# Key/value projection third, queries five tiles ahead, transposes moved, norm gains as rows, FFN2's first split behind the norm

## The chip, the cores and the metric

The kernel runs on one core of a Trainium2 chip. The metric is the device time of one execution in microseconds (us); three runs of the kernel before gave a median of 1015.74 us (1014.93 to 1016.44). The engines are TensorE (PE, its weight loads PEld), VectorE (DVE), ScalarE (ACT), GpSimd (POOL) and SyncE (SP), which here issues nearly all DMAs. Each engine works through its own instructions in order.

## The reference

One encoder layer over 512 tokens of width 1024, all in float32:

```
x = x + 0.5 * swiglu(rms_norm(x, ffn1_norm), gate1, up1, down1)     # width 2816
h = rms_norm(x, mix_norm);  P = h @ w_in                            # q, k, v of A and B
A: 8 heads of differential attention, two softmaxes each over 512 keys, + T5 bias, RMS norm
B: 8 query heads over 2 key/value heads, per-head RMS norm and rotary on q and k, softmax
x = x + concat(A, B) @ w_out
x = x + 0.5 * swiglu(rms_norm(x, ffn2_norm), gate2, up2, down2)
return rms_norm(x, final_norm)
rms_norm(x, g) = x * rsqrt(mean(x*x) + 1e-6) * g
```

## The kernel before

**Arithmetic.** Every large operand is split into two fp32r parts, hi (a cast on ScalarE) and lo (the difference, a subtraction on VectorE), and a product is three matmuls: hi by hi, hi by lo, lo by hi (`mm3`). A split of a weight block thus is ScalarE and VectorE work that has to be done before TensorE can use it; `Blocks` holds the list of weight blocks, loads them two ahead through SP (`load`) and splits them (`convert`, `get`). Evicting a transposed activation from PSUM is such a split too.

**Stages.** FFN1's gate/up products (0 to 246.7 us) go over 11 blocks of 256 columns; from the second on each product is made of seven smaller ones with sums of sub-blocks: of weights (T, on GpSimd and VectorE) and of activations (S1 to S4, `left_sums`). Then come FFN1's down product (to 366.4), the mix norm and the first projections (to 411), attention (to about 632), the output projection and FFN2's norm (to 660), FFN2's gate/up (to 884), down (to 1001) and the final norm.

**Norms.** A norm handles 128 tokens at a time: ScalarE's Square with its sum, VectorE and GpSimd for r, then z = x·r on VectorE (128x1024), eight transposes of 128x128 on TensorE per tile, into four PSUM banks, and the eviction of 128x256 pieces: hi with the column's gain as the scale on ScalarE, lo on VectorE. The gains of the three norms are loaded as columns (`gcol`, 4-byte elements) through SP at the start. `left_first` does the first 256 tokens, `left_second` the others.

**Attention.** 32 units of A and 32 of B, one for a head and 128 queries, named A0_0 to A7_3 and B0_0 to B7_3. The loop at the end of `build` takes one unit a step and is a software pipeline: scores of unit i (sA, sB), the join of softmax parts of unit i-1, the transposes of the weights (pt_A, pt_B) of unit i-3 (`LAG_T`), the product with v (poA, poB) of unit i-4 or i-5 (`LAG_V`), and for A the transposes of a head pair's output (ot) 7 units behind (`LAG_O`). The order of TensorE's instructions in the loop is that of the code. Between these steps `fill` puts other matmuls, "fillers", of which `FILLS` gives how many groups of three go to a step (one number for eight steps): first the projections in the order `FILL_ORDER`, then the output projection (po), which needs the ot tiles. For B, `B_heads` transposes a head's rotated queries (hT_q), splits them and copies them to the other 64 partitions by DMAs on SP (qh, ql), three steps ahead of the head's first unit; `make_k2` does the same for the keys (hT_k). The q and k of a head pair of A are copied into stacks (st) by small DMAs on SP. Outside the loop a scheduler orders the instructions of each engine by the code's order and by modelled costs; `tc.issue_after(x)` keeps instructions behind x.

Of the kernel before, what the change touches and what calls it, by code (L numbers as in the profile page):

```python
# [155 lines left out]
def build(ctx, tc, a, out):  # L156
# [100 lines left out]
    gcol = {}  # L257
    for nm in ("ffn1", "mix", "ffn2"):
        gcol[nm] = const.tile([P, NK], F32, name=f"gcol_{nm}")
        nc.sync.dma_start(out=gcol[nm], in_=a[f"{nm}_norm"][0].rearrange("(k p) -> p k", p=P))  # L260
        if nm == "ffn1":
            for t in (2, 3):
                nc.sync.dma_start(out=xn[t], in_=xv[:, t, :])
            blocks.load(2)
# [30 lines left out]
    def half_T(half, tags, tag, between=None, parts=2):  # L295

        ps = [bank(tags[kp], f"xt_{tag}{half}{kp}") for kp in range(4)]
        for i in range(2):
# [8 lines left out]
        return [(p.rearrange("p (k s) -> p k s", k=2)[:, e, :]) for p in ps for e in range(2)]  # L307

    def gained(hl, e, p, gain):

        last["act"] = nc.scalar.activation(hl[0][:, e, :], p, AF.Copy, scale=gain).ins
        last["dve"] = nc.vector.scalar_tensor_tensor(out=hl[1][:, e, :], in0=p, scalar=gain,
                                              in1=hl[0][:, e, :].bitcast(F32), op0=ALU.mult, op1=ALU.subtract).ins
# [4 lines left out]
    def left_first(g, tag, between=None, parts=2):  # L318

        ps = half_T(0, "DDBB", tag, between, parts)  # L320
# [738 lines left out]
```

## Time and profile before

| | |
|---|---|
| median of 3 runs | 1015.74 us (1014.93 to 1016.44) |
| profiled execution, its own time | 1015.6 us |
| span, first to last instruction | 1013.8 us |
[...]
| busy: PE, DVE, ACT, POOL | 974.1 (96%), 720.6 (71%), 489.0 (48%), 227.9 (22%) us |
| chain that ended last | PE 83%, DVE 6%, issue 3%, ACT 2%, DMA 2% |

TensorE is busy 96% of the span; the list of its waits and the timeline show the rest. A row of the timeline has the start, the duration, the engine, the line, the operation, its output and inputs and in brackets the idle time of the engine before it with what ended it. Line numbers are those of the kernel before.

### The profile page before, as it was taken

The page shows a single profiled execution, that of the slowest core. Times are in us where ns is not written, and L with a number is a line of the kernel's source. Part 1 is how long each engine was busy: PE and PEld are TensorE (multiplying, and loading weights), DVE is VectorE, ACT ScalarE, POOL GpSimd, SP SyncE. Part 2 cuts the span into 40 slices and gives each one's busy share as a digit, 9 for nine tenths or more (in the row PEclk, how much of TensorE's full clock was granted, in tenths as well). Part 3 has the DMA queues.
Part 4 walks back from the last instruction along what each step waited for, and adds up shares of the span by engine and source line. Part 5 has one row for each costly group of instructions (what it writes and reads, how often), then busy time and mean ns, then how long its engine had stood idle before and what let it go on. Part 6 is the DMA issues. An engine that isn't in the chain of part 4 may idle for free.

```text
span 1013.8 us, 16666 instructions
## 1 busy us (share of the span) xinstructions
PE 974.1 (96%) x6540; PEld 893.7 (88%) x6540; DVE 720.6 (71%) x1156; ACT 489.0 (48%) x845; POOL 227.9 (22%) x222
## 2 busy tenths in 40 slices
PE   7999999999999999999899989899999999999995
PEld 7999999999888888799888777699999999988884
DVE  5998899988232173777988886689999887842224
ACT  7555444445231162776766665574444454622213
POOL 1232223220000000122656442033222323000001
PEclk8999999999999999999999999999999999999998
DMA  8145534323223325545412121114433423233212
GB/s 244 52 127 188 179 108 126 116 93 109 99 83 106 102 79 144 139 116 158 136 54 58 27 63 52 43 42 125 126 103 106 126 83 125 84 111 118 83 42 83
DMA packets 82399, 105.45 MB, mean 104 GB/s; under 512 B 7873, under 2 KB 66753, under 8 KB 82321
## 3 DMA queue, kind: packets, MB, share of 16 engines
q1 hardware_dynamic: 81744, 103.35, 33.1%
q8 instruction: 51, 0.84, 0.4%
q10 hardware_dynamic: 576, 1.05, 0.3%
q14 instruction: 28, 0.22, 0.1%
HBM read 93.86 MB, written 6.32 MB: 99 GB/s over the span
## 4 chain that ended last, share of the span: by engine, by line
PE 83%; DVE 6%; issue 3%; ACT 2%; DMA 2%; POOL 2%; SPq 1%; POOLq 0%; DVEq 0%; ACTq 0%
PE dn L217 23%; PE bg L217 6%; PE cu L217 6%; PE dg L217 6%; PE du L217 6%; PE bu L217 6%; PE cg L217 6%; PE po L217 3%; PE pqk L217 3%; PE au L217 3%; PE ag L217 3%; PE pva L217 2%; PE poA L217 2%; PE poB L217 1%; PE g L217 1%
## 5 line engine op out<-in xcount | busy, mean ns | idle before, releaser
L102 DVE TENSOR_TENSOR lo_d<-raw_d,hi_d 128x1024 fp32r<-128x1024 f32 x44 | 52.2, 1219 | 84.9 <-ACT hi_d L101 84.9
L132 POOL TENSOR_TENSOR T_g<-raw_g 128x512 f32<-128x512 f32 x40 | 69.1, 1727 | 156.8 <-DVE tl_u L102 75.7
L101 ACT CAST hi_d<-raw_d 128x1024 fp32r<-128x1024 f32 x44 | 44.1, 1051 | 89.8 <-PE dn L217 87.3
L132 POOL TENSOR_TENSOR T_u<-raw_u 128x512 f32<-128x512 f32 x40 | 55.0, 1374 | 128.4 <-DVE tl_g L102 88.9
L101 ACT CAST th_u<-T_u 128x512 fp32r<-128x512 f32 x60 | 37.2, 620 | 88.8 <-PE bg L217 44.6
L101 ACT CAST th_g<-T_g 128x512 fp32r<-128x512 f32 x60 | 37.0, 620 | 46.6 <-PE cu L217 26.5
L758 ACT ACTIVATE s_A<-s_A,m_A 128x512 f32<-128x512 f32 x64 | 45.9, 721 | 25.3 <-DVE m_A L756 25.2
L102 DVE TENSOR_TENSOR lo_g<-raw_g,hi_g 128x1024 fp32r<-128x1024 f32 x44 | 55.7, 1272 | 1.0 <-ACT hi_g L101 0.9
L101 ACT CAST hi_g<-raw_g 128x1024 fp32r<-128x1024 f32 x44 | 44.7, 1047 | 23.6 <-PE dg L217 11.4
L102 DVE TENSOR_TENSOR tl_u<-T_u,th_u 128x512 fp32r<-128x512 f32 x60 | 54.7, 912 | 0.0
L102 DVE TENSOR_TENSOR lo_u<-raw_u,hi_u 128x1024 fp32r<-128x1024 f32 x44 | 53.2, 1216 | 1.6 <-ACT hi_u L101 1.4
L102 DVE TENSOR_TENSOR tl_g<-T_g,th_g 128x512 fp32r<-128x512 f32 x60 | 52.6, 879 | 0.0
L101 ACT CAST hi_u<-raw_u 128x1024 fp32r<-128x1024 f32 x44 | 44.3, 1052 | 15.0 <-PE du L217 12.1
L756 DVE CUSTOM_DVE_ANT_0 s_A<-sA,T 128x512 f32<-128x512 f32 x64 | 42.0, 684 | 9.5 <-PE sA L217 7.5
L829 POOL TENSOR_TENSOR p_B<-p_B,m_B 128x512 f32<-128x512 f32 x32 | 34.5, 1083 | 38.3 <-DVE m_B L828 30.9
L217 PE MATMUL pqk<-xm,hi_qk 128*128 128x512 f32 x128 | 40.3, 396 | 0.0
L217 PEld LDWEIGHTS poA<-va,PT_A 128*128 128x128 f32 x256 | 32.4, 195 | 3.7 <-ACT PT_A L720 3.1
L274 POOL TENSOR_TENSOR r_fin<-r_fin,mhalf 128x1 f32<-128x1 f32 x4 | 2.5, 638 | 145.4 <-DVE r_fin L273 145.4
L217 PE MATMUL poA<-va,PT_A 128*128 128x64 f32 x256 | 33.0, 273 | 2.2 <-ACT PT_A L720 2.2
L274 POOL TENSOR_TENSOR r_mx<-r_mx,mhalf 128x1 f32<-128x1 f32 x4 | 2.2, 552 | 145.0 <-DVE r_mx L273 145.0
L439 ACT ACTIVATE g<-g 128x1024 f32<-128x1024 f32 x20 | 21.2, 1061 | 18.3 <-DVE g L437 18.2
L217 PE MATMUL pqb<-hi_qb,xm 128*128 128x256 f32 x128 | 29.3, 298 | 0.0
(667 smaller groups left out, 3765.3 us busy)
## 6 DMA issues: line engine op xcount, KB each, us to landing
raw_d<-ffn_w_down SPq DMA_DIRECT2D x22, 1024.0 KB, 4.9
raw_g<-ffn_w_gate SPq DMA_DIRECT2D x21, 1024.0 KB, 5.5
raw_u<-ffn_w_up SPq DMA_DIRECT2D x21, 1024.0 KB, 5.4
toep<-nbd SPq DMA_DIRECT2D x8, 512.0 KB, 8.5
raw_qk<-w_in SPq DMA_DIRECT2D x8, 512.0 KB, 4.7
raw_o<-w_out SPq DMA_DIRECT2D x4, 1024.0 KB, 5.5
T<-toep SPq DMA_DIRECT2D x8, 448.0 KB, 4.1
xn<-x SPq DMA_DIRECT2D x4, 512.0 KB, 4.6
```

The costliest lines, as they stand in the source:

```text
L101: self.nc.scalar.copy(out=hi, in_=src)
L102: self.nc.vector.tensor_sub(lo, src, hi.bitcast(F32))
L132: eng.tensor_sub(b12 if n == 1 else T[n], x, T[2] if n == 4 else y)
L217: i = nc.tensor.matmul(*args, **kw)
L274: last["pool"] = nc.gpsimd.tensor_tensor(out=r, in0=r, in1=mhalf[:, 0:1], op=ALU.pow).ins
L439: nc.scalar.activation(g1, g1, AF.Silu)
L756: nc.vector.tensor_tensor_reduce(out=sc, in0=ps, in1=T[:, 384 - P * qt:896 - P * qt], scale=1.0, scalar=BIG, op0=ALU.add, op1=ALU.min, acc ...
L758: nc.scalar.activation(sc, sc, AF.Exp, bias=m[:, s:s + 1], scale=-1.0, accum_out=l1[:, qt, h:h + 1] if s == 0 else l2)
L829: nc.gpsimd.tensor_mul(u["P"], u["P"], l.to_broadcast([P, S]))
```

## The change

There are six parts.

1. The gains of the mix norm and of FFN2's norm are loaded as rows repeated on all partitions (G, 128x1024) and multiplied in with z (`scalar_tensor_tensor`, x·r·G). The evictions then need no scale, so two 128x256 pieces become one of 128x512. FFN1 keeps its columns, loaded through ScalarE's DMA queue.
2. The key/value projection is the third filler, not the fifth, and `make_k2` stands after eight groups of qb0, not fifteen.
3. `FILLS` has one number for four steps.
4. The transposes of A's outputs stand 9 units behind, not 7, and the queries of B's heads are transposed five steps ahead (`LEAD_B`), of the first head three.
5. At the start of both FFNs: raw copies of the activations stand behind the last eviction of the first half, the second half behind the last of these copies, the first split of gate weights behind z, and the splits of S1 to S4 behind the main split of the second gate block.
6. FFN2's norm begins after the third of the last four output blocks, not the second, and the next weights are only loaded there.

```diff
-FILL_ORDER = ("qk1", "qk2", "va1", "qk3", "kv", "qb0", "qb1")
+FILL_ORDER = ("qk1", "qk2", "kv", "va1", "qk3", "qb0", "qb1")
-FILLS = (3.0, 3.0, 3.0, 2.6, 1.3, 1.1, 1.1, 1.1, 2.0)
+FILLS = (3.0, 3.0, 3.0, 3.0, 3.0, 3.0, 3.0, 2.2, 1.0) + 7 * (1.2,) + (1.4, 1.4)
-LAG_O = 7
+LAG_O = 9
+LEAD_B = (3, 5, 5, 5, 5, 5, 5, 5)
...
+    gcol = const.tile([P, NK], F32, name="gcol")
+    nc.scalar.dma_start(out=gcol, in_=a["ffn1_norm"][0].rearrange("(k p) -> p k", p=P))
...
-            nc.vector.tensor_scalar_mul(z, xn[t], r)
+            if G is None:
+                i = nc.vector.tensor_scalar_mul(z, xn[t], r)
+            else:
+                i = nc.vector.scalar_tensor_tensor(out=z, in0=xn[t], scalar=r, in1=G, op0=ALU.mult, op1=ALU.mult)
+            last["z"] = i.ins
...
+    def evict(hi, lo, p, kp, G):
+
+        for e, col in pieces(kp, G):
+            last["act"] = plain_copy(hi[:, e, :], p[:, e, :], col).ins
+            if col is None:
+                last["dve"] = nc.vector.tensor_sub(lo[:, e, :], p[:, e, :], hi[:, e, :].bitcast(F32)).ins
...
+        for kp, n, e in quarters(("A11", "A12")):
+            evict(L[n][0][:, e, :], L[n][1][:, e, :], ps[kp], kp, G)
+        with tc.issue_after(last["act"]):
+            for kp, n, e in quarters(("A11", "A12")):
+                for e_, col in pieces(kp, G):
+                    plain_copy(raw[n][:, e, :][:, e_, :], ps[kp][:, e_, :], col)
...
+        with tc.issue_after(last["act"]):
+            ps = half_T(1, "BCDD", tag, G, None, parts)
...
+    def left_splits(L, raw, tag):
+        for n in ("S2", "S1", "S3", "S4"):
             L[n] = pair_of(f"{n}{tag}")
+            blocks.parts(L[n][0], L[n][1], raw[n])
...
-        w["g"] = blocks.get(at["g", i, 0], further=False)
+        with tc.issue_after(last["z"]):
+            w["g"] = blocks.get(at["g", i, 0], further=False)
...
+        with tc.issue_after(blocks.main):
+            left_splits(L, raw, f"f{i + 1}")
...
+            whi, wlo = blocks.get(at[("o", part, hh)], further=(part, hh) != (1, 1))
+            if (part, hh) == (1, 1):
+                blocks.load(at["u", 1, 0] + 1)
...
-                if part == 1 and hh == 1 and t0 == 1:
+                if part == 1 and hh == 1 and t0 == 2:
                     st["half_done"]()
...
-                if nm == "qb0" and w == 15:
+                if nm == "qb0" and w == 8:
                     make_k2()
...
-        rate = FILLS[i // 8]
+        rate = FILLS[i // 4]
...
+        for head, lead in enumerate(LEAD_B):
+            if i != n // 2 + NT * head - lead:
+                continue
             need(lambda: len(k2) == 2 and all((head // 4, t) in qn for t in range(NT)))
             B_heads(head)
+            if head == 7:
+                G2 = rows_of(xgpool, "ffn2", tag="xg", bufs=NXG)
```

How the order of the instructions changes is shown at three places. The first is ScalarE at the start of FFN1: z_f10 to z_f13 are the Squares of the four token tiles, hi_g00 the first gate block, A11f1h and A12f1h the evictions of the first half's transposes. Before:

```order
L292 ACTIVATE z_f11_139,ss_f11_140<-xn1_96 128x1024
L101 CAST hi_g00_193<-raw_g00_101 128x1024 x2
L292 ACTIVATE z_f12_259,ss_f12_260<-xn2_97 128x1024
L311 ACTIVATE A11f1h_157<-xt_f100_117,gcol_ffn1_104 128x256
L311 ACTIVATE A11f1h_157<-xt_f101_118,gcol_ffn1_104 128x256
L292 ACTIVATE z_f13_274,ss_f13_275<-xn3_98 128x1024
L311 ACTIVATE A12f1h_160<-xt_f102_119,gcol_ffn1_104 128x256
L311 ACTIVATE A12f1h_160<-xt_f103_120,gcol_ffn1_104 128x256
```

and of the change:

```order
L102 CAST hi_g00_189<-raw_g00_103 128x1024 x2
L324 ACTIVATE A11f1h_153<-xt_f100_113,gcol_99 128x256
L324 ACTIVATE A11f1h_153<-xt_f101_114,gcol_99 128x256
L324 ACTIVATE A12f1h_156<-xt_f102_115,gcol_99 128x256
L324 ACTIVATE A12f1h_156<-xt_f103_116,gcol_99 128x256
...
L324 ACTIVATE A12f1h_156<-xt_f103_116,gcol_99 128x256
L292 ACTIVATE z_f12_255,ss_f12_256<-xn2_97 128x1024
L292 ACTIVATE z_f13_270,ss_f13_271<-xn3_98 128x1024
L102 CAST hi_u00_243<-raw_u00_108 128x1024
```

The eight evictions now follow hi_g00, and the Squares of the tiles 2 and 3 (z_f12, z_f13) stand behind them all.

The second is TensorE in attention, at the transposes of the keys (hT_k0, from the rotated keys kn0 to kn3); pqb01 and pqb00 are the projections of B's queries, pkv0 that of its keys and values. Before:

```order
L217 MATMUL pqb01_5249<-lo_qb0_4917,xm7_3698 128x256
L217 MATMUL pqb01_5249<-hi_qb0_4916,xm7_3698 128x256
L217 MATMUL sA6_00_5376<-st_kqk30_4888,st_qqk30_4884 128x512
L217 MATMUL sA6_01_5381<-st_kqk31_4896,st_qqk31_4892 128x512
L222 MATMUL hT_k0_5393<-ident_72,kn0_5223 64x128
L222 MATMUL hT_k0_5393<-ident_72,kn1_5239 64x128
L222 MATMUL hT_k0_5393<-ident_72,kn2_5054 64x128
L222 MATMUL hT_k0_5393<-ident_72,kn3_5070 64x128
```

and of the change, first where pkv0 ends, then where hT_k0 stands:

```order
L224 MATMUL pt_A1_3_4636<-ident_72,pm_A1_3_4492 128x128 x4
L219 MATMUL pkv0_4530<-hi_kv_4149,xm6h_3695 128x256
L219 MATMUL pkv0_4530<-lo_kv_4150,xm6h_3695 128x256
L219 MATMUL pkv0_4530<-hi_kv_4149,xm6l_3696 128x256
L219 MATMUL pva11_4686<-hi_va1_4354,xm0h_3689 128x256
...
L224 MATMUL pt_A4_3_5290<-ident_72,pm_A4_3_5142 128x128 x4
L224 MATMUL hT_k0_5298<-ident_72,kn0_4660 64x128
L224 MATMUL hT_k0_5298<-ident_72,kn1_4676 64x128
L224 MATMUL hT_k0_5298<-ident_72,kn2_4512 64x128
L224 MATMUL hT_k0_5298<-ident_72,kn3_4528 64x128
```

pkv0 now ends ahead of the scores of A2_3, and hT_k0 stands between the weights' transposes of A4_3 and the scores of A5_3; before, the projection ended in A5_1 and hT_k0 stood behind the scores of A6_0.

The third is VectorE at FFN2's norm: po4 to po7 are the last output blocks, z_f20 to z_f22 the normalized tiles, lo_g10 and lo_u10 the first splits of FFN2's weights, A11f2l and A12f2l the splits of the evicted first half. Before:

```order
L916 TENSOR_TENSOR xn3_98<-po1_3_6847,xn3_98 128x512
L102 TENSOR_TENSOR lo_g10_6894<-raw_g10_6761,hi_g10_6893 128x1024 x2
L916 TENSOR_TENSOR xn0_95<-po1_4_6901,xn0_95 128x512
L271 TENSOR_TENSOR r_f20_6937<-ss_f20_6934 128x1
L916 TENSOR_TENSOR xn1_96<-po1_5_6915,xn1_96 128x512
L273 TENSOR_SCALAR r_f20_6937<-r_f20_6937 128x1
L301 TENSOR_SCALAR z_f20_6933<-xn0_95,r_f20_6937 128x1024
L271 TENSOR_TENSOR r_f21_6954<-ss_f21_6951 128x1
L273 TENSOR_SCALAR r_f21_6954<-r_f21_6954 128x1
L301 TENSOR_SCALAR z_f21_6950<-xn1_96,r_f21_6954 128x1024
L916 TENSOR_TENSOR xn2_97<-po1_6_6997,xn2_97 128x512
L312 SCALAR_TENSOR_TENSOR A11f2l_6968<-xt_f200_6929,gcol_ffn2_113,A11f2h_6967 128x256
```

and of the change:

```order
L959 TENSOR_TENSOR xn0_95<-po1_4_6879,xn0_95 128x512
L271 TENSOR_TENSOR r_f20_6929<-ss_f20_6926 128x1
L273 TENSOR_SCALAR r_f20_6929<-r_f20_6929 128x1
L305 SCALAR_TENSOR_TENSOR z_f20_6925<-xn0_95,r_f20_6929,G_ffn2_6548 128x1024
L959 TENSOR_TENSOR xn1_96<-po1_5_6893,xn1_96 128x512
L271 TENSOR_TENSOR r_f21_6946<-ss_f21_6943 128x1
L273 TENSOR_SCALAR r_f21_6946<-r_f21_6946 128x1
L305 SCALAR_TENSOR_TENSOR z_f21_6942<-xn1_96,r_f21_6946,G_ffn2_6548 128x1024
L103 TENSOR_TENSOR lo_g10_6998<-raw_g10_6738,hi_g10_6997 128x1024 x2
L959 TENSOR_TENSOR xn3_98<-po1_7_6977,xn3_98 128x512
L331 TENSOR_TENSOR A11f2l_6960<-xt_f200_6921,A11f2h_6959 128x512
L331 TENSOR_TENSOR A11f2l_6960<-xt_f201_6922,A11f2h_6959 128x512
```

lo_g10 went from ahead of the additions of po1_4 and po1_5 to behind z_f21, where it stands ahead of the A11f2l splits.

## Rows read from the trace of the kernel before

**Rows 1.** stretches: length, busy us of engines (count), PEclk, DMA share, GB/s.
```profile
0.00:17.50 17.50, 12.41 (x50) 9.96 (x51) 8.78 (x18) 11.73 (x21) 2.91 (x10) 0.86 0.81 241
...
45.00:86.80 41.80, 41.75 (x342) 40.86 (x343) 40.10 (x53) 18.65 (x26) 11.77 (x8) 1.00 0.42 128
...
366.40:376.30 9.90, 8.31 (x54) 7.49 (x53) 6.82 (x18) 7.09 (x21) 1.10 (x2) 0.83 0.06 23
...
411.00:450.00 39.00, 37.42 (x255) 33.58 (x254) 29.00 (x80) 26.92 (x62) 8.39 (x15) 1.00 0.48 131
...
490.00:530.00 40.00, 35.20 (x270) 33.19 (x269) 35.30 (x97) 26.22 (x64) 23.71 (x33) 0.96 0.33 91
530.00:570.00 40.00, 35.32 (x234) 30.21 (x234) 34.04 (x79) 26.53 (x61) 22.98 (x26) 1.00 0.17 44
```

**Rows 2.** TensorE's waits: us in total, times, longest.
```profile
PE hT_k L222 <- DVE kn L685: 3.6, 2, 3.2
PE g L217 <- ACT A11f1h L311: 3.2, 1, 3.2
PE ot L222 <- DVE o L798: 2.5, 1, 2.5
PE sB L217 <- DMA qh<-qh: 2.4, 2, 1.9
PE xt_f L304 <- DVE r_f L271: 2.4, 1, 2.4
PE bg L217 <- DVE lo_g L102: 2.3, 2, 1.9
...
PE po L217 <- ACT otB L101: 1.4, 1, 1.4
```

**Rows 3.** timeline, TensorE behind hT_k: start us, us, engine, line, what.
```profile
505.02 0.63 PE L217 MATMUL pqb<-hi_qb,xm 128*128 128x256 f32 x2
...
508.48 0.28 PE L217 MATMUL pqb<-lo_qb,xm 128*128 128x256 f32 x1
508.60 0.40 PE L217 MATMUL pqb<-hi_qb,xm 128*128 128x256 f32 x2
```

**Rows 4.** timeline, start of FFN1.
```profile
8.65 4.18 SPq L260 DMA_DIRECT2D gcol_ffn<-ffn_norm  x1
...
8.99 1.05 ACT L101 CAST hi_g<-raw_g 128x1024 fp32r<-128x1024 f32 x1 [0.65 <-DMA raw_g<-ffn_w_gate]
...
11.45 1.06 ACT L292 ACTIVATE z_f<-xn 128x1024 f32<-128x1024 f32 x1 [1.41 <-DMA xn<-x]
...
12.51 0.82 ACT L311 ACTIVATE A11f1h<-xt_f,gcol_ffn 128x256 fp32r<-128x256 f32 x2
```

**Rows 5.** tiles z_f, S2rf: count, ns min/median/max, first and last start.
```profile
L292 ACT ACTIVATE z_f<-xn x12: 614/642/1061, 4.4 to 659.4; 128x512 f32<-128x512 f32 x8, 128x1024 f32<-128x1024 f32 x4
...
L301 DVE TENSOR_SCALAR z_f<-xn,r_f x8: 745/753/1768, 6.5 to 661.2; 128x1024 f32<-128x1024 f32 x8
...
L351 DVE TENSOR_TENSOR S2rf<-S1rf,A11rf x2: 1215/1762/2310, 30.0 to 671.7; 128x1024 f32<-128x1024 f32 x2
```

**Rows 6.** evictions at the mix norm (timeline), and 128x512 ones (groups).
```profile
373.69 3.82 ACT L311 ACTIVATE xm<-xt_mx,gcol_mix 128x256 fp32r<-128x256 f32 x10 [1.29 <-PE xt_mx L304]
...
374.20 3.26 DVE L312 SCALAR_TENSOR_TENSOR xm<-xt_mx,gcol_mix,xm 128x256 fp32r<-128x256 f32 x8 [1.22 <-ACT xm L311]
...
L615 ACT ACTIVATE qk00h<-pqk x1: 599/599/599, 391.1 to 391.1; 128x512 fp32r<-128x512 f32 x1
```

**Rows 7.** timeline of VectorE at FFN2's norm.
```profile
639.84 2.35 DVE L102 TENSOR_TENSOR lo_g<-raw_g,hi_g 128x1024 fp32r<-128x1024 f32 x2
642.11 0.68 DVE L916 TENSOR_TENSOR xn<-po,xn 128x512 f32<-128x512 f32 x1
```

**Rows 8.** an issue of a stack DMA (timeline), and their landing (DMA view).
```profile
480.83 0.59 SPq L625 DMA_DIRECT2D st_qqk<-qk30l  x1
...
st_kqk<-qk31h SPq DMA_DIRECT2D x8, 64.0 KB, 2.0
```

More of the change, by code (lines that the diff above doesn't have):

```diff
@@ L256, in build @@
     blocks.load(1)
[L257 to L264, printed above, removed]
+    for t in (2, 3):
+        nc.sync.dma_start(out=xn[t], in_=xv[:, t, :])
+    blocks.load(2)
     def rsqrt(ss, tag):
@@ L293, in root, with half_T @@
         return rsqrt(ss[:, :parts], f"{tag}{t}"), z
-    def half_T(half, tags, tag, between=None, parts=2):
+    def half_T(half, tags, tag, G=None, between=None, parts=2):
         ps = [bank(tags[kp], f"xt_{tag}{half}{kp}") for kp in range(4)]
@@ L306, in half_T, with pieces, plain_copy, quarters @@
                 between()
[L307 to L313, printed above, removed]
+        return [p.rearrange("p (k s) -> p k s", k=2) for p in ps]
+    def pieces(kp, G):
+        if G is not None:
+            return [(slice(0, 2), None)]
+        return [(slice(e, e + 1), gcol[:, 2 * kp + e:2 * kp + e + 1]) for e in range(2)]
+    def plain_copy(out, p, col):
+        if col is None:
+            return nc.scalar.copy(out=out, in_=p)
+        return nc.scalar.activation(out, p, AF.Copy, scale=col)
+    def evict(hi, lo, p, kp, G):
+        for e, col in pieces(kp, G):
+            last["act"] = plain_copy(hi[:, e, :], p[:, e, :], col).ins
+            if col is None:
+                last["dve"] = nc.vector.tensor_sub(lo[:, e, :], p[:, e, :], hi[:, e, :].bitcast(F32)).ins
+            else:
+                last["dve"] = nc.vector.scalar_tensor_tensor(
+                    out=lo[:, e, :], in0=p[:, e, :], scalar=col, in1=hi[:, e, :].bitcast(F32),
+                    op0=ALU.mult, op1=ALU.subtract).ins
     def pair_of(name):
         return [xgpool.tile([P, 4, 256], F32R, tag="xg", name=f"{name}{w}", bufs=NXG) for w in "hl"]
[L318 to L320 removed]
+    def quarters(names):
+        return [(kp, names[kp // 2], slice(2 * (kp % 2), 2 * (kp % 2) + 2)) for kp in range(4)]
+    def left_first(G, tag, between=None, parts=2):
+        ps = half_T(0, "DDBB", tag, G, between, parts)
         L, raw = {}, {}
@@ L574, in keep_warm @@
             nc.tensor.matmul(pw, warm[:, :P], warm, start=True, stop=True)
-    L, raw, second = first_half(gcol["ffn1"], "f1", keep_warm, 1)
+    L, raw, second = first_half(None, "f1", keep_warm, 1)
     H = gate_up(0, L, raw, second, small_things)
-    xg = []
+    G_mix = rows_of(fpool, "mix", tag="ut", bufs=1)
+    xg, xm = [], []
     def mix_half(half):
         if not xg:
-            for k in range(NK):
-                t = xgpool.tile([P, 2, S], F32R, tag="xg", name=f"xm{k}", bufs=NXG)
-                xg.append((t[:, 0, :], t[:, 1, :]))
+            for k in range(0, NK, 2):
+                hl = [xgpool.tile([P, 2, S], F32R, tag="xg", name=f"xm{k}{w}", bufs=NXG) for w in "hl"]
+                xg.extend((hl[0][:, e, :], hl[1][:, e, :]) for e in range(2))
+                xm.append(hl)
         s = slice(256 * half, 256 * half + 256)
-        for k, p in enumerate(half_T(half, "DDBB", "mx")):
-            gained([x_[:, None, s] for x_ in xg[k]], 0, p, gcol["mix"][:, k:k + 1])
+        for kp, p in enumerate(half_T(half, "DDBB", "mx", G_mix)):
+            hi, lo = xm[kp]
+            evict(hi[:, :, s], lo[:, :, s], p, kp, G_mix)
     down(0, H, lambda t: mix_half(t // 2) if t % 2 else None)
```

58 lines of the change are left out of this document (26 added, 32 removed).

## The prediction

> **What bounds it now.** The table by stretches comes first: in the long FFN stretches TensorE is busy nearly all the time (from 45.0 to 86.8 us 41.75, beside 40.10 on VectorE), so nothing is to be had there but by fewer matmuls, and the change takes none away. TensorE is idle where stages meet: in the first 17.5 us, at a granted clock of 0.86, and from 490 to 570, 35.20 and 35.32 busy of 40 each [rows 1]. Then the list of TensorE's waits says who ended each: the key transposes (hT_k) 3.6 us, the first gate matmuls (g) 3.2, the transposed outputs (ot) 2.5, sB behind a DMA of queries 2.4, the transposes of FFN2's norm (xt_f) 2.4, bg behind lo_g 2.3, po behind otB 1.4 [rows 2]. [...] The edits aim at these waits; each is a few us of 1015.6.
>
> **The change part by part** (a gain is positive; of the profiled execution, 1015.6, that is the span of 1013.8 and 1.8 around it, 0.14 under the median of 1015.74).
>
> 1. *Start of FFN1.* ScalarE now evicts the first normalized half directly behind hi_g. Before, the Square of xn[2] stood between, which began at 11.45 after 1.41 us of waiting for its DMA; A11h began at 12.51 and g half a microsecond later. hi_g ends at 8.99 + 1.05 = 10.04, so A11h and with it g can begin nearly 2.5 earlier [rows 4]. At the top, a shorter pause also spares half of what the low clock costs in the first 17.5 us, (1 - 0.86) x 17.5 = 2.5 [rows 1]: 3.8 in all. At the bottom it is 0, since the Squares of xn[2] and xn[3] now wait behind eight evictions, half of hi_u behind eight raw copies, and VectorE is 96% busy until 86.8. I take **2.0**, nearer to the row that moves.
>
> 2. *lo_g ahead of the S splits.* In each FFN's second block lo_g stood among the splits of S1 to S4, and bg waited 2.3 for it in two waits, 1.9 of them in FFN2 [rows 2]. The splits now come late instead; TensorE has the rest of ag and bg to do before it needs them. **1.9**, between 0 and 2.3.
>
> 3. *Gain rows at the mix norm.* z = x·r·G reads two tensors. No such 128x1024 instruction is in the trace; its neighbours are z now, 0.75, and a subtraction of two tensors of that size, 1.22 beside a quiet GpSimd and 2.31 beside a working one [rows 5]. GpSimd does little at both norms, so I take 1.22: 0.47 more per tile. Evictions go from eight to four per half: on ScalarE ten took 3.82, so eight 3.06, against four at 0.60 (128x512 from PSUM), 0.66 less; on VectorE eight took 3.26, against four at 0.68 (such an addition), 0.54 less [rows 6, 7]. The first eviction is longer, so pva starts later, and 31 pva matmuls stand now ahead of the second tile's transposes. **0.7**, from -1.2 (two z's and the first eviction) to 2.5 (the 1.6 idle of 9.90 us at the norm, and half of the 1.7 that its clock of 0.83 costs [rows 1]).
>
> [...]
>
> 4. *Key/value projection third, keys transposed earlier.* pkv now ends in unit A2_3 and hT_k stands in A5_3, 12 units on; before, it stood right behind its rotary work. The wait goes, 3.6 in all [rows 2], and with it the half clock of [rows 3]: 0.96 granted from 490 to 530 is 0.04 x 40 = 1.6 lost [rows 1]. The cover is 12 units of 3.3 (the 66 steps of attention fill 411 to 632), 40 us. **5.2**; 3.2 if the clock is lost elsewhere and a small wait stays.
>
> 5. *Queries five units ahead.* The two sB waits on the landing of qh are 2.4 together, the longest 1.9 [rows 2]; two units more are over 6 us of lead. **2.4**, between 0 and 2.4.
>
> 6. *Outputs' transposes two units later.* ot waited 2.5 for o [rows 2]. But out_proj's first block needs ot_3, which now comes two units later, with the fillers ahead of it used up; the po right behind it must wait for ot's eviction, some 0.6 on ScalarE and 0.7 on VectorE by the neighbours in [rows 6, 7]. And VectorE is busy 34.04 of 40 there [rows 1]. **0.5**, from -1 (a longer queue) to 2.8 (both waits gone).
>
> 7. *FFN2's start.* Nine matmuls of output block 6 stand now ahead of the wait for otB, 1.4, and cover it: 9 x 0.24 = 2.2, at twice the 0.12 by which a pair of 256 columns takes longer than one (0.40, 0.28 [rows 3]). lo_g (2.35) is no longer ahead of the addition that the norm needs, which began as it ended, at 642.11 [rows 7]; z comes about 1.2 earlier, less 0.47, and three matmuls fewer (0.7) lie ahead of the transposes: the wait of 2.35 becomes about 1.1. lo_g now stands between z and the A11l splits on VectorE, for which g waits: those are 2.35 later, which po's last block (12 x 0.24 = 2.9) and the transposes cover for the most part; I charge 1.0. 1.4 + 1.2 - 1.0 = **1.6**, from 0 to 3.6.
>
> 8. *Cost: pair 3's stacks.* pqk31 now ends three units before sA6_00, not eight. Such a unit holds 27 filler matmuls at 0.12 and some 0.85 of its own: 12.2 in all. Behind pqk31 come hi_qb (the casts of a block, 2 x 1.05, as hi_g [rows 4]) and lo_qb behind each (the last 1.22, by the neighbour in [rows 5]), and qk31l, 0.7: 4.0, and 5.0 with what those engines have in hand. A raw_o load stands on SP's queue behind lo_qb and ahead of seven stack DMAs, each 0.59 to issue and 2.0 to land [rows 8]: 5.0 + 4.1 + 2.0 = 11.1. One us of slack, on engines four fifths busy: **-1.5**, between 0 and -3.
>
> 9. *Column gains on ScalarE's queue.* The issue of such a load held SP for 4.18 [rows 4]; on ScalarE, begun at 1, it can hold up the first Square, at 4.4 [rows 5], by up to 0.8: **-0.4**, between 0 and -0.8. The two such loads that leave SP and the two gain rows cost nothing: nothing in FFN1's start waits for SP then, and the rows have tens of us until they are read.
>
> Sum: 2.0 + 1.9 + 0.7 + 5.2 + 2.4 + 0.5 + 1.6 - 1.5 - 0.4 = 12.4, so 1015.6 - 12.4 = **1003.2**.
>
> **Rivals.**
> *A. VectorE sets the pace of attention.* It is busy 35.30 and 34.04 of 40 from 490 to 570, as long as TensorE [rows 1]; a queue that full passes the removed waits on. Terms 5 and 6 and half of 4 come back: 12.4 - 2.4 - 0.5 - 2.6 = 6.9, or 1008.7. Against it: the k/v work moves to about 420 to 450, and of 411 to 450 VectorE is busy only 29.00 of 39.
> *B. The starts give nothing.* z at 1.22 and above, lo_g ahead of A11l, the second half's Squares late: terms 1 and 7 at 0, term 3 at -1.2: 12.4 - 2.0 - 1.6 - 1.9 = 6.9, again 1008.7. For it speaks that ScalarE and VectorE do there about what they did, in another order.
> *C. Slower: query preparation ahead of the softmax.* With five units of lead each head's rotary work on VectorE may stand ahead of the maximum for which TensorE waits. If each of the eight heads costs one stall as long as the longest on its queries now, 1.9 [rows 2], that is 8 x 1.9 = 15.2: 1018.4. It makes the kernel slower from 12.4 / 8 = 1.6 per head on. Against it: the same work is done now, and none of the six largest waits is on a maximum [rows 2].
> *D. No net change.* If the rate at which fillers are handed out (3.0 until unit 27) leaves TensorE without any around ot_3, idle there can undo terms 4, 5 and more, up to 12: about 1015. Now 4.7 of 40 is idle from 530 to 570.
>
> **How the numbers follow.** Forecast 0.62; A 0.16; B 0.11; C 0.06; D 0.05. All low ends together give 1018, all high ends 993; they are separate places, so about half of either reach is likely: 997 to 1007 for the forecast, and to 1011 to take in A and B with their spread. 0.2%, 2 us, is about what a measurement can tell from no change. Faster 0.87 (the forecast, A and B less their tails), same 0.06, slower 0.07.
>
> **What would show it.** Right: g begins before 11.5; no hT_k wait, and full clock from 490 to 530; no sB wait on qh; no bg wait above 0.5; no otB wait. Wrong: an sA wait on st_kqk above 3 us at unit A6_0 (term 8); po or ot waits above 2.5 between 530 and 570 (term 6, D); waits of about 2 us on a maximum, once per head (C); z at 2.3 (B). If the first block's gain is eaten by 86.8 us, new gaps on hi_u or on the S splits show it.

## The result, and the profile after

The changed kernel takes **1002.71 us** (median of 4 runs, 1002.07 to 1003.15) against 1015.39 for the kernel before in the same session (4 runs): a ratio of **0.9869, 95% interval 0.9858 to 0.9881**. Forecast were 1003.2 and a range of 997 to 1011. The profiled execution took 1002.5, with a span of 1000.7 instead of 1013.8. TensorE's busy time fell by only 4.6 (974.1 to 969.5); its idle gaps of 0.1 us and more fell from 29.3 to 21.0. Both kernels do 6540 matmuls, so the gain is waits and half clock (a granted clock of 0.50, as from 504.40 to 507.60 behind hT_k in the kernel before; the mean over the span rose from 0.988 to 0.992), no work taken away.

First the table by stretches (columns as in [rows 1]), each stretch at the place of the program that its row of before shows; the last one is FFN2's norm.

```profile
0.00:17.50 17.50, 12.98 (x54) 10.61 (x55) 9.18 (x22) 11.67 (x20) 2.36 (x9) 0.83 0.92 294
...
45.00:86.80 41.80, 41.80 (x345) 40.91 (x344) 41.63 (x51) 18.03 (x27) 16.04 (x8) 1.00 0.33 103
...
363.90:376.30 12.40, 10.72 (x84) 9.66 (x83) 7.51 (x14) 6.06 (x16) 1.10 (x2) 1.00 0.05 19
...
487.00:526.00 39.00, 35.56 (x288) 33.84 (x287) 37.08 (x89) 26.46 (x66) 19.35 (x26) 1.00 0.40 109
526.00:564.00 38.00, 33.81 (x223) 28.56 (x222) 33.54 (x78) 25.92 (x58) 23.47 (x28) 1.00 0.18 49
...
621.00:647.00 26.00, 22.89 (x112) 19.07 (x111) 16.72 (x28) 13.13 (x29) 1.10 (x2) 0.93 0.13 42
```

The granted clock of 0.96 in the middle of attention is 1.00 now. VectorE is busier there than TensorE, 37.08 of 39 against 35.56; that it is the next limit there no run tests. Two of these stretches are still below full clock, the start (0.83) and FFN2's norm (0.93).

TensorE's waits after (columns as in [rows 2]):

```profile
PE poA L219 <- ACT PT_A L761: 2.3, 3, 1.6
PE sA L219 <- DVE m_A L797: 2.1, 2, 1.6
PE xt_f L309 <- DVE z_f L303: 2.0, 2, 1.6
PE sB L219 <- ACT p_B L864: 1.9, 2, 1.2
PE g L219 <- DVE A11f2l L331: 1.8, 1, 1.8
PE po L219 <- ACT ot L771: 1.7, 1, 1.7
...
PE xt_f L309 <- DVE z_f L305: 1.2, 1, 1.2
...
PE ag L219 <- DVE lo_g L103: 0.9, 1, 0.9
...
PE sA L219 <- DMA st_kqk<-qk31h: 0.6, 1, 0.6
```

The waits on hT_k, ot, qh, bg and otB [rows 2] are all off the list. New are g behind A11f2l, 1.8, and at the start xt_f behind z, 1.6; po behind ot's eviction has grown from 0.3 to 1.7.

Where the gain arose shows when the same instruction of TensorE is looked up in both traces: the first down product starts 2.4 earlier, the first sA of attention 3.6, the last down matmul 13.1. From the first sA to the transposes of FFN2's norm 7.0 are gained, although 12 po matmuls more (12 x 0.23 = 2.8) are done by then; 2.5 of these 9.8 are the otB wait and the shorter xt_f wait, which belong to term 7. That leaves 7.3 for attention itself, and 13.1 - 3.6 - 7.3 = 2.2 for FFN2's start.

| place (terms) | predicted | measured |
|---|---|---|
| FFN1 (1, 9) | 1.6 | 2.4 |
| mix norm (3) | 0.7 | 1.2, clock (below) |
| attention (4, 5, 6, 8) | 6.6 | 7.3 |
| FFN2's start (7, 2) | 3.5 | 2.2 |

The start of FFN1 on ScalarE (timeline):

```profile
0.74 0.46 ACTq L258 DMA_DIRECT2D gcol<-ffn_norm  x1
...
7.26 1.06 ACT L292 ACTIVATE z_f<-xn 128x1024 f32<-128x1024 f32 x1 [1.52 <-DMA xn<-x]
...
11.19 0.83 ACT L324 ACTIVATE A11f1h<-xt_f,gcol 128x256 fp32r<-128x256 f32 x2
```

A11h starts at 11.19 instead of 12.51 [rows 4], 1.3 earlier, not nearly 2.5. The Square of xn[1] waits 1.52 for its load until 7.26; in the trace of before it began at 5.80. FFN2's norm, VectorE:

```profile
634.26 1.28 DVE L305 SCALAR_TENSOR_TENSOR z_f<-xn,r_f,G_ffn 128x1024 f32<-128x1024 f32 x1 [0.66 <-POOL r_f L274]
...
639.15 2.35 DVE L103 TENSOR_TENSOR lo_g<-raw_g,hi_g 128x1024 fp32r<-128x1024 f32 x2
641.42 0.68 DVE L959 TENSOR_TENSOR xn<-po,xn 128x512 f32<-128x512 f32 x1
642.02 1.28 DVE L331 TENSOR_TENSOR A11f2l<-xt_f,A11f2h 128x512 fp32r<-128x512 f32 x2
```

And TensorE behind it:

```profile
642.75 0.39 PE L219 MATMUL g<-A11f2l,hi_g 128*128 128x256 f32 x1 [1.85 <-DVE A11f2l L331]
...
644.76 0.41 PE L219 MATMUL g<-A11f2h,lo_g 128*128 128x256 f32 x1
644.98 0.41 PE L219 MATMUL g<-A11f2h,hi_g 128*128 128x256 f32 x1
...
647.71 0.28 PE L219 MATMUL g<-A12f2h,lo_g 128*128 128x256 f32 x1
```

lo_g no longer stands ahead of the norm, but ahead of A11f2l. After that wait the matmuls start 0.22 apart and take 0.41 (half clock), from 646.6 on 0.12 and 0.28.

### The profile page after: what moved, and what is told of

The parts are those of the page before. It is cut to its first block, busy times and chain, and to the rows that moved or that the text cites. A ratio compares the mean times of both kernels' runs of the same rounds, so it can differ in the third digit from the quotient of the medians.

```text
span 1000.7 us, 16625 instructions
## 1 busy us (share of the span) xinstructions
PE 969.5 (97%) x6540; PEld 891.0 (89%) x6540; DVE 727.4 (73%) x1138; ACT 481.7 (48%) x823; POOL 236.5 (24%) x222
## 4 chain that ended last, share of the span: by engine, by line
PE 84%; DVE 7%; DMA 3%; issue 2%; ACT 2%; POOL 2%; SPq 1%; POOLq 0%; DVEq 0%; ACTq 0%
PE dn L219 24%; PE bg L219 5%; PE cg L219 5%; PE cu L219 5%; PE bu L219 5%; PE dg L219 5%; PE du L219 5%; PE po L219 3%; PE pqk L219 3%; PE ag L219 3%; PE au L219 3%; PE g L219 3%; PE u L219 2%; PE poA L219 1%; DMA gb_k<-k_norm 1%
## 5 line engine op out<-in xcount | busy, mean ns | idle before, releaser
L133 POOL TENSOR_TENSOR T_g<-raw_g 128x512 f32<-128x512 f32 x40 | 78.0, 1950 | 146.4 <-DVE tl_u L103 75.4
L102 ACT CAST hi_u<-raw_u 128x1024 fp32r<-128x1024 f32 x44 | 44.6, 1050 | 15.7 <-PE du L219 10.0
L219 PE MATMUL po<-hi_o,ot 128*128 128x512 f32 x64 | 26.7, 417 | 1.8 <-ACT ot L771 1.7
L864 ACT ACTIVATE p_B<-sB,m_B 128x512 f32<-128x512 f32 x32 | 22.1, 691 | 11.3 <-DVE m_B L861 8.9
```

Of the source, the lines that this page charges most:

```text
L133: eng.tensor_sub(b12 if n == 1 else T[n], x, T[2] if n == 4 else y)
L219: i = nc.tensor.matmul(*args, **kw)
L864: nc.scalar.activation(pm, ps, AF.Exp, bias=m[:, 0:1], scale=1.0, accum_out=m[:, 1:2])
```

## Experiments

The change is the base unless said otherwise, and the ratio is always to the kernel before of the same session (medians 1016.07 to 1016.8); the change itself stands at 0.9869. "Attention" is the time from the first sA to the first transposes of FFN2's norm in the profiled execution, against the change. Five other profiled executions with the change's order of TensorE's instructions in attention lie between -0.4 and +1.2, so that is how far one such number can be off. The largest of them (starts, experiment 9) has half clock behind po's wait for ot's eviction, where the change has the same wait and full clock (rows at the end).

**1. k and v fifth again** (kv_fifth)

```diff
-FILL_ORDER = ("qk1", "qk2", "kv", "va1", "qk3", "qb0", "qb1")
+FILL_ORDER = ("qk1", "qk2", "va1", "qk3", "kv", "qb0", "qb1")
-                if nm == "qb0" and w == 8:
+                if nm == "qb0" and w == 15:
```

> The change, with the key/value projection fifth among the fillers and the key transposes behind its fifteenth group again. If the waits add up one by one (the working of the prediction), the hT_k wait of 3.6 us and about 1.6 us of half clock come back between 490 and 530, and the new wait of 0.6 on st_kqk goes: 4.6 slower than the change, 1007.3. If VectorE sets the pace of attention, at most half of that comes back: below 1005.3.

Measured: 1006.58, ratio 0.9901 [0.9881, 0.9922]; attention +4.6. TensorE at the key transposes:

```profile
500.56 1.70 PE L224 MATMUL hT_k<-ident,kn 128*64 128x128 f32 x7 [3.22 <-DVE kn L726]
501.91 0.56 PE L219 MATMUL pqb<-hi_qb,xm0h 128*128 128x256 f32 x1
...
502.91 0.41 PE L219 MATMUL pqb<-lo_qb,xm0h 128*128 128x256 f32 x1
```

The old wait returns with its half clock (0.41 a matmul, not 0.28; 0.80 granted over the 8 us from 500.56). But that is not all of the 4.6. A second stretch of half clock, 0.79 over the 8 us from 561.67, follows po's wait for ot's eviction (1.49), which the change has too (1.71), there at full clock. And TensorE's idle gaps in attention grow by only 1.3 in all, since other waits shrink as hT_k's comes back. So term 4 is a wait and a stretch of half clock as the prediction said, but that the 4.6 equals the expected sum is in part luck.

**2. Queries three ahead again** (lead3)

```diff
-LEAD_B = (3, 5, 5, 5, 5, 5, 5, 5)
+LEAD_B = (3, 3, 3, 3, 3, 3, 3, 3)
```

> The change, with the queries of every head of B transposed three units ahead again. If the waits add up, the two sB waits on the landing of qh come back, 2.4 us: 1005.1. If another wait only stood behind them (sB on p_B, 1.9 in the change), less than 1 us comes back: below 1003.7.

Measured: 1006.96, 0.9905 [0.9885, 0.9926]; attention +3.9. One wait on qh comes back, and the table by stretches shows what follows it, here and in the change:

```profile
575.00:600.00 25.00, 22.79 (x115) 18.01 (x114) 18.06 (x36) 15.48 (x34) 9.91 (x10) 0.93 0.31 85
```

```profile
575.00:600.00 25.00, 25.00 (x136) 20.53 (x135) 22.29 (x46) 19.41 (x43) 13.30 (x11) 1.00 0.32 90
```

The wait is 2.05 at 584.68; 0.07 x 25 = 1.75 is lost to the clock around it. Together 3.8. Before the change no half clock followed this wait (1.91 at 593.01, 1.00 granted over the 8 us behind it).

**3, 4. Outputs' transposes 7 and 8 units behind** (lago7, lago8)

```diff
-LAG_O = 9
+LAG_O = 7      # lago8: 8
```

> The change, with the outputs of A transposed seven units behind again. The working of the prediction gives this edit 0.5 us: 1003.2, with the ot wait on o of about 2.5 back and the po wait on ot of 1.7 gone. The rival, that the later transposes free VectorE and bring the whole of 2.5, gives 1005.2; that they cost more than they bring (fillers used up) gives 1002.0 or less.

> The change, with the outputs of A transposed eight units behind, between the seven of before and the nine of the change. At seven TensorE reached ot at 549.8 and waited 3.8 for o, whose time is set by VectorE's queue, and fell to half clock; at nine it does not wait for o. If the time of o stands and only TensorE's arrival moves, by one step of some 2.4 us, the wait on o is 1.4, not long enough to lose the clock, and the po wait on ot stays below 1: 1.0 above the change or less, 1002.7 to 1003.7. If every step counts, half of the 4.4 us of lag seven: 1005.

Measured: lago7 1006.69, 0.9908 [0.9886, 0.993], attention +4.9; lago8 1003.21, 0.9871 [0.9848, 0.9893], attention +0.5. The transposes of the fourth output in lago7:

```profile
549.18 0.66 PE L224 MATMUL pt_B<-ident,p_B 128*128 128x128 f32 x4 [0.33 <-POOL p_B L870]
553.62 1.09 PE L224 MATMUL ot<-ident,o 128*128 128x128 f32 x4 [3.78 <-DVE m_B L869]
```

and VectorE ahead of them:

```profile
551.60 0.67 DVE L861 TENSOR_REDUCE m_B<-sB 128x1 f32<-128x512 f32 x1
552.20 0.67 DVE L882 TENSOR_TENSOR PTl_B<-pt_B,PTh_B 128x512 fp32r<-128x512 f32 x1
552.80 0.67 DVE L839 TENSOR_TENSOR o<-o,of 128x512 f32<-128x512 f32 x1
```

The o that ot needs is a multiplication at 552.80, in VectorE's queue behind maxima and splits without a gap. (The trace puts the end of the wait down to the reciprocals m_B beside it; but ot starts 0.15 after o ends, as it does in experiment 5, 0.14, where o itself is named.) TensorE is there at 549.84 and waits 3.78, more than before the change (2.5 [rows 2]); experiment 5 shows why. Half clock follows (0.90 granted from 540 to 575). One unit of lag is enough to step past it: none of lago8's waits of 1.3 and more is on o. So lago8 does not show whether 1.4 there would have cost clock; behind otB's 1.36 at 635.06 in the kernel before the clock stayed at 1.00, behind po's 1.45 in starts it did not (rows at the end). What the second unit gives, 0.5, is within what executions differ by.

**5. All three undone, with the old fill rates** (attn_undone: the diffs of 1 to 3 and that of 6)

> The change, with all of its edits of attention undone together: key/value projection fifth, queries three ahead, outputs seven behind, the fillers handed out as before. Undone one at a time, three of them gave back 4.4, 4.5 and 4.4 us of span. If the waits are separate, these add up to 13.3: 1016. If each edit only pays as long as the others stand (a queue of VectorE that shifts its delay to whichever instruction is next), together they give back what attention has gained by the comparison of the two traces, 6.6 to 7.0: 1009.5, with the waits on kn, o and qh of the kernel before and no longer ones.

Measured: 1010.01, 0.9937 [0.9916, 0.9958]; attention +7.75, half of what the same edits cost singly (4.6 + 3.9 + 4.9 + 2.3 = 15.7, the last from experiment 6). The medians of all runs say less sharply the same: by the ratios, singly 3.2, 3.7, 4.0 and 1.6 against the change, 12.5 in all, together 6.9, each with an interval of about 2. Waits:

```profile
PE hT_k L224 <- DVE kn L726: 3.7, 2, 3.2
PE ot L224 <- DVE o L839: 2.5, 1, 2.5
...
PE sB L219 <- DMA qh<-qh: 1.9, 1, 1.9
```

After the hT_k wait TensorE reaches ot at 554.00, 4.2 later than in lago7, and ot starts at 556.48, 2.9 later. A wait removed upstream is paid in part at the next one.

What does not add up, though, is mostly the clock. TensorE's idle gaps of 0.1 us and more in attention grow by 1.3, 1.3, 2.0 and 0.4 singly (5.0) and by 4.4 together; what the granted clock takes away (one less its mean, times the stretch) is 3.4, 1.7, 3.4 and 1.7 singly (10.2), 3.4 together, and 0 in the change. Part of that clock is chance, as in experiments 1 and 9; how much of it the runs do not separate.

**6. Old fill rates alone** (fills_old)

```diff
-FILLS = (3.0, 3.0, 3.0, 3.0, 3.0, 3.0, 3.0, 2.2, 1.0) + 7 * (1.2,) + (1.4, 1.4)
+FILLS = (3.0, 3.0, 3.0, 2.6, 1.3, 1.1, 1.1, 1.1, 2.0)
-        rate = FILLS[i // 4]
+        rate = FILLS[i // 8]
```

> The change, with the fillers handed out as before (one rate for eight steps). The prediction gave this edit no term of its own. If it is only a way to share out the same work, the same time within 1 us: 1002 to 1003.7. If the fillers run out elsewhere, a wait on the softmax parts between 480 and 570 grows and 1 to 3 us are lost: 1004 to 1006.

Measured: 1004.42, 0.9885 [0.9869, 0.9901]; attention +2.3, poA's waits on PT_A 3.6 instead of 2.3, and half clock behind the longest of them (2.03; 0.79 granted over the 8 us from 512.90), where the change has 1.60 and full clock. The intervals of the two ratios overlap. The prediction gave this edit no term.

**7. k and v third in the kernel before** (kv_alone: the diff of 1 reversed, nothing else of the change)

> The kernel before with one edit of the change alone: key/value projection third, key transposes behind the eighth group. If the waits are separate, the 3.6 us on kn and 1.6 of half clock go: 5.2 less, 1010.2. If an edit pays only together with the others (undone one at a time, three of them gave back 13.3, all together 7.7), this one brings half or less, 1012.8 or more, and a longer wait on ot or qh shows instead.

Measured: 1012.71, 0.9973 [0.9958, 0.9987]. Attention is 2.0 shorter than before, not 5.2. Its waits:

```profile
PE sB L217 <- ACT p_B L823: 2.1, 3, 1.2
PE po L217 <- ACT otB L101: 2.0, 1, 2.0
PE sA L217 <- DVE m_A L756: 2.0, 2, 1.6
PE ot L222 <- DVE m_B L828: 1.7, 1, 1.7
```

The hT_k wait shrinks to 1.1, the wait on qh is gone and ot's is shorter, so the longer wait on ot or qh that was expected did not come. But sB behind p_B grows from 1.2 to 2.1 and po behind otB from 1.4 to 2.0, and the half clock has only moved: 1.00 is granted from 480 to 520 and 0.96 from 520 to 560, behind ot; before, it was 0.96 and 1.00. Alone the edit brought less than half of its price; as in experiment 5, what it brings depends on the others.

**8. S splits ahead of the main split** (splits)

```diff
+            left_splits(L, raw, f"f{i + 1}")
             blocks.convert(at["g", i, 1] + 1)
-        with tc.issue_after(blocks.main):
-            left_splits(L, raw, f"f{i + 1}")
```

> The change, with the splits of S1 to S4 ahead of the main split of each FFN's second gate block again. By the working of the prediction the bg waits on lo_g come back, 1.9 in FFN2 and 0.4 in FFN1: 2.3 slower, 1005.0. If the order on VectorE only decides which operand is late, less than 0.7 us: 1003.4 or less.

Measured: 1005.22, 0.9892 [0.9872, 0.9912]. In FFN2 the wait is back, +2.1 by the second block:

```profile
672.12 0.39 PE L219 MATMUL bg<-A12f2h,lo_g 128*128 128x256 f32 x1 [1.84 <-DVE lo_g L103]
```

In FFN1 it costs 0.4.

**9. Raw copies and second half in the old order** (starts; at both places)

```diff
-        with tc.issue_after(last["act"]):
+        if True:
```

> The change, with the raw copies and the second half's norm free to go ahead of the first half's evictions again, in both FFNs (the gate split stays behind z, the S splits behind the main split). By the working of the prediction g begins 2 to 2.5 us later in FFN1, as ScalarE waits for the DMA of xn[2] first, and half of it or more stays: 1 to 2.5 slower, 1003.7 to 1005.2. The rival is that VectorE, busy all of 45 to 86.8, takes it back: the same time as the change at the 48th bg matmul and in all, 1002.7.

Measured: 1004.72, 0.9887 [0.9871, 0.9903]. TensorE at the start (timeline):

```profile
7.80 0.60 PE L309 MATMUL xt_f<-ident,z_f 128*128 128x128 f32 x4
9.95 1.10 PE L309 MATMUL xt_f<-ident,z_f 128*128 128x128 f32 x8 [1.55 <-DVE z_f L303]
13.06 0.80 PE L219 MATMUL g<-A11f1h,hi_g 128*128 128x256 f32 x2 [2.01 <-ACT A11f1h L324]
```

g starts 1.35 later than in the change (13.06 against 11.71); of this 0.41 is left at 86 us and nothing at the first down product: near 115 VectorE waits for the load of a rotary gain in the change (1.17, here 0.79), and TensorE has a wait of 0.9 on lo_g at 123 that is not there in this kernel. In FFN2 the old order costs 2.7, more than the 1.6 of term 7. The rest of what this kernel loses is attention, +1.2 with the same order of instructions: half clock behind po's wait for ot's eviction (1.45).

**10. Gain columns at the mix norm and FFN2's** (cols)

```diff
-    G_mix = rows_of(fpool, "mix", tag="ut", bufs=1)
+    G_mix = cols["mix"]
...
-    st["half_done"] = lambda: begun.extend(first_half(G2, "f2"))
+    st["half_done"] = lambda: begun.extend(first_half(cols["ffn2"], "f2"))
```

> The change, with the gains of the mix norm and of FFN2's norm as columns at the eviction again (two column loads on SP at the start, 128x256 evictions, z without a gain). The working of the prediction gives the rows 0.7 us at the mix norm, the trace of the change 1.2, most of it from a clock that no longer falls there: 1003.4 to 1003.9 in all, with a granted clock of 0.83 again in the 10 us at the mix norm. If the longer z (1.22 against 0.75 us, four times on the path) is what counts, columns are the faster way: 1001.0 to 1002.0.

Measured: 1004.57, 0.9877 [0.9855, 0.9899], span of the profiled execution 1000.5: no difference to the change that the intervals show. The mix norm in this kernel:

```profile
363.50:375.90 12.40, 10.67 (x83) 9.52 (x81) 9.41 (x24) 10.64 (x26) 1.10 (x2) 1.00 0.01 3
```

and in lago8, whose instructions there are those of the change:

```profile
363.51:375.91 12.40, 10.88 (x75) 10.11 (x74) 6.63 (x12) 4.58 (x13) 1.10 (x2) 0.86 0.06 23
```

lago8 does 75 matmuls in these 12.4 us and the change 84 (1.00 in the table by stretches): the clock there differs between executions of identical instructions. It was 0.83 before [rows 1] and 1.00 in kv_alone, again with the same instructions. From the first xt_mx to the 96th pva this is 18.67 (change) against 20.08 (lago8) with rows, 18.10 (kv_alone; 17.89 in cols) against 19.00 (before) with columns. At equal clock rows are 0.6 to 1.1 slower there; by the first sA nothing is left of it (159.4 us behind the first down product in the change, 159.5 in cols and 159.7 in kv_alone; 160.6 before). Of the 1.2 in the table above 0.9 to 1.1 is thus the clock.

**11. Three repairs** (best1): FFN1's gains loaded as eight rows of 128 and transposed by TensorE; lo_g in halves, one ahead of the last addition and one behind the A1 splits; the rotary tables' instructions two blocks later.

```diff
-    nc.scalar.dma_start(out=gcol, in_=a["ffn1_norm"][0].rearrange("(k p) -> p k", p=P))
+    nc.scalar.dma_start(out=g8, in_=a["ffn1_norm"][0].rearrange("(k p) -> k p", p=P))
...
+    nc.tensor.transpose(pg[:, :NK], g8, ident[:NK, :NK])
+    nc.vector.tensor_copy(gcol, pg[:, :NK])
...
+        else:
+            w["g"] = blocks.get_halves(at["g", i, 0], lambda h: tc.issue_after(last["dve"] if h else last["add1"]))
...
+        if j == 5:
```

> The change with three additions. (a) FFN1's gains are loaded as 8 rows of 128 and transposed on TensorE, in place of 1024 packets of 4 bytes. If these packets are what made xn[1] land late in the change (its Square began at 7.26, before at 5.80), the second tile's transposes begin 1.3 us sooner, near 8.75. If ScalarE's queue or anything else delays it, they stay near 10.1. (b) The first half of FFN2's lo_g goes between the addition of the second tile and its norm, the second half behind the A11 and A12 splits. The g wait on A11f2l (1.85) should go, and with it the half clock behind it, 1.4: about 3 us less. (c) The rotary tables are built two blocks later; the wait of 0.9 on lo_g at 123.3, behind a VectorE that waits for the DMA of k_norm, should go. In all 4 to 5 us less: 998.0 to 999.0; only (b) and (c): 999.5; none: 1002.7.

Measured: 999.11, 0.9831 [0.9816, 0.9847]. The start, and FFN2's second half (timeline):

```profile
5.71 1.06 ACT L312 ACTIVATE z_f<-xn 128x1024 f32<-128x1024 f32 x1
...
10.51 0.50 PE L235 MATMUL g<-A11f1h,hi_g 128*128 128x256 f32 x2 [0.60 <-ACT A11f1h L344]
...
645.74 1.06 PE L329 MATMUL xt_f<-ident,z_f 128*128 128x128 f32 x8 [1.70 <-DVE z_f L325]
```

The Square of xn[1] starts at 5.71 without a wait and g at 10.51: the load in single floats was what held it (7.13 to 7.29 in all ten kernels with that load on ScalarE's queue, 5.71 and 5.84 in best1 and best2). The wait at 123 is gone. FFN2's norm runs at 1.00 from 618 to 644 without the g wait, but the second half's z is late now (1.70), and by FFN2's first down product 0.1 is left of what the split in halves won. Of the 3.2 that the profiled executions differ by, 2.9 are there at FFN1's first down product: the gain is that of the start.

**12. And FFN2's first up split behind the second half's norm** (best2)

```diff
...
+            first = [last[e] for e in ("act", "dve", "pool")]
+            second()
+            with ExitStack() as es:
+                for x_ in (*first, last["z"]):
+                    es.enter_context(tc.issue_after(x_))
+                w["u"] = blocks.get(at["u", i, 0], further=False)
...
```

> The kernel best1 with one more edit: in FFN2's first block the split of the first up weights (hi_u, lo_u) stands behind the norm of the last two token tiles, not ahead of it. In best1 the wait on A11f2l went, but 0.9 of the gain of 1.2 was lost again by a wait of 1.7 on z_f of the third tile, which stood behind lo_u (2.36) on VectorE. If that is the cause, z_f comes some 1.5 us sooner and the total is 1.0 to 1.5 below best1: 997.6 to 998.1. If lo_u is then late for the up matmuls by as much, nothing is won: 999.1.

Measured: **996.21** (996.01 to 997.77), 0.9804 [0.979, 0.9817], the fastest of all, faster than both kernels, and 2.9 below best1 where 1.0 to 1.5 were expected. From the transposes of FFN2's norm to its first down product 3.1 are gained on the change, where best1 had 0.1. The stretch with the second half's transposes, in best1:

```profile
644.00:670.00 26.00, 23.68 (x196) 23.27 (x196) 22.29 (x24) 16.74 (x25) 7.54 (x6) 1.00 0.23 74
```

and in best2, with TensorE busy throughout:

```profile
644.00:670.00 26.00, 26.00 (x220) 26.00 (x220) 24.81 (x28) 18.57 (x28) 8.08 (x4) 1.00 0.37 120
```

## Why the prediction was right, point by point

The sum came out within 0.5 us, but not every term did, and that it came out so near is in part luck: errors of about 1 to 2 us in single places cancelled.

- *Term 1 and 9 (FFN1's start, 2.0 and -0.4).* The reordering did what was said at g: undone, it costs 1.35 there. g began at 11.71, not before 11.5. But by the first down product nothing of it is left: the kernel starts reaches it at 244.00, the change at 244.11, the kernel before at 246.50. So the 2.4 gained in FFN1 does not come from an earlier g, and that it lies near the 1.6 of these terms is luck. In both kernels TensorE's waits between 42 and 45 us are gone (bu on H 0.9, du on hi_u 0.4, bg on lo_g 0.4), of which the prediction counted bg's alone, in term 2. At g itself the mis-sized term is 9. Its cost was sought in ScalarE's issue, which takes 0.46; it is the arrival of xn[1], 1.46 later. That is why g gained 1.3 instead of nearly 2.5. That the scattered load holds up the other one was shown by taking it away (best1: the Square at 5.71 instead of 7.26); how it does so no run shows. On the way 0.9 was lost at 123 us.
- *Term 2 (1.9).* Right: 2.1 in FFN2 and 0.4 in FFN1 when undone.
- *Term 3 (0.7).* z took 1.28 for the 1.22 assumed. That 1.22 [rows 5] is not beside a quiet GpSimd: this S2rf starts at 671.66, and GpSimd works on T_g from 671.27 to 675.16. The figure holds all the same: with GpSimd idle, subtractions of that size take 1.21 to 1.23 in the same trace (S4rf at 35.13: 1.21). But rows are slower, not faster, in the first projections, and level by attention (cols): the fewer evictions only just pay for the longer z. Most of the 1.2 gained there is the clock of one execution: of the same instructions the change does 84 matmuls in 12.4 us at 1.00, lago8 75 at 0.86.
- *Terms 4, 5, 6 (5.2, 2.4, 0.5).* Each wait went. Undone one at a time they cost 4.6, 3.9 and 4.9; together with the fill rates 7.75. So the terms have no size of their own: a wait upstream delays TensorE's arrival at the next, and half clock comes or stays away behind the same wait. Term 6 was too small for a reason: it counted ot's wait as it was before, 2.5, and not as it would be (3.78 and half clock) once hT_k no longer delayed TensorE. Term 5 left out half clock behind its wait; none stood there before, 1.75 did in lead3. In the sum (8.1, less 1.5 for term 8: 6.6, measured 7.3) this hardly shows, which is luck: the change's profiled execution has no half clock in attention at all, others with its order do.
- *Rival A (VectorE's pace)* has its mechanism confirmed and its price refuted: VectorE sets when o is ready, but moving the transposes past that moment avoids it. In kv_alone more than half of what the edit should gain is taken back, but at waits that end on ScalarE (p_B, otB) as well as on VectorE, and by the clock.
- *Term 7 (1.6).* otB's wait went and xt_f's fell from 2.35 to 1.24, as worked out. The charge of 1.0 for lo_g ahead of A11l was too small: 1.85 of wait and, by 15 matmuls 0.09 further apart, 1.4 of half clock. This is the term that made FFN2's start 2.2 instead of 3.5. The half clock in it is again that of an execution: of eight kernels with this wait (1.83 to 1.86) five show it, while kv_fifth, lago7 and fills_old keep 1.00 and reach FFN2's first down product 0.6 to 0.7 sooner after the norm's transposes. Before, half clock stood behind the xt_f wait of 2.35 instead (0.79 granted over the 8 us from 646.29), which the term did not count as a gain.
- *Term 8 (-1.5).* The wait on st_kqk is 0.6. The sum of 11.1 against 12.2 was short on one side: in the change pqk31 ends at 484.75, the last stack lands 13.3 later and TensorE is there 12.8 later. The stack DMAs issued behind raw_o took up to 4.7 to land (issued at 492.52, landed at 497.20), not 2.0. The charge of 1.5 covered it.
- *Fill rates.* No term; undone they cost 2.3 in attention, part of it half clock (experiment 6).
- *Rivals B, C, D* did not come: z is at 1.27 to 1.29 seven times out of eight, and once, at FFN2's last tile, at 2.32, the 2.3 that B named; waits on m_A are 2.1 in all, in two places and not once per head (1.9 before), and none is on m_B; and where D expected TensorE to run out of fillers its longest wait is 1.7 (po behind ot).

What stays open: how often half clock follows one and the same wait. Only profiled executions show it, one of each kernel. At the mix norm it came in two of eleven with rows (lago8, best2) and in one of three with columns (before), so up to 1.4 of the 12.7 us between the medians may be this; the waits in attention and at FFN2's g come on top.

## What to carry to other kernels

Look behind a wait for the half clock that may follow it, and price both where TensorE will arrive once the waits ahead of it are gone, not as the profile of before has it. Whether a wait of 1.4 to 2.5 us costs clock one profile does not tell (po's 1.71 in the change did not, its 1.45 in starts did); several executions of one order do. Edits of one in-order pipeline are to be tried together as well as singly: here singles undone summed to twice the whole, and one applied alone gave less than half of its term. When a piece of work is moved off one critical chain, look at what it now stands ahead of. Splitting it (lo_g in halves) removed the wait behind it, but paid only when lo_u, the next in the way, was moved too (best2).

## What the runs showed of the hardware

- The load of 4 KB in single floats, issued on ScalarE's queue, delayed the 512 KB load of xn[1] on SP's by 1.5 us (Square at 7.26 in the change; at 5.71 in best1, with the same 4 KB as eight rows).
- The granted clock at the same instructions differed from execution to execution: 1.00 (change) or 0.86 (lago8) over 12.4 us at the mix norm, 0.9 to 1.4 us of time.
- Half clock followed a wait of TensorE in one execution and not in another. The three waits on hT_k of 3.2 us (before, kv_fifth, attn_undone) and that of 3.78 on ot (lago7) were all followed by it. Of the shorter ones some were and some were not: po behind ot's eviction in the change (1.71) and in starts (1.45), g in kv_fifth (1.83; the change's 1.85 was), ot before (2.47; attn_undone's 2.48 was). The 8 us behind the wait in the change, starts, kv_fifth and before, in this order, with the clock as the third number from the end:

```profile
558.05:566.05 8.00, 7.94 (x42) 6.36 (x43) 6.59 (x14) 4.23 (x10) 2.47 (x3) 1.00 0.07 16
557.08:565.08 8.00, 7.94 (x35) 6.29 (x36) 5.15 (x11) 3.29 (x8) 2.07 (x3) 0.79 0.00 0
647.76:655.76 8.00, 7.43 (x61) 7.25 (x62) 7.42 (x11) 5.35 (x14) 2.99 (x3) 1.00 0.73 237
559.60:567.60 8.00, 7.64 (x40) 5.74 (x41) 5.32 (x11) 3.93 (x10) 3.65 (x4) 1.00 0.00 1
```

- What such a stretch cost was not its lost clock alone: 0.79 over 8 us is 1.7 less clock, and attention grew by 1.2 in starts, but not at all in best2 (half clock behind a poA wait of 1.71, attention 0.3 shorter than in the change).
- z with a second tensor took 1.27 to 1.29 on VectorE in the six cases with GpSimd idle. Of the last two, one row of 3.52 in the timeline, the first took 1.28 and the second, from 648.88 on, 2.32; GpSimd works on T_g from 648.11 to 650.11, beside the end of the first too. Nor did work on GpSimd go with the longer time in each case of the kernel before: the subtraction S2rf took 2.31 beside it at 30.05 and 1.22 beside it at 671.66. The row of the last two:

```profile
647.67 3.52 DVE L305 SCALAR_TENSOR_TENSOR z_f<-xn,r_f,G_ffn 128x1024 f32<-128x1024 f32 x2 [0.58 <-POOL r_f L274]
```
